# Split-SiLU-multiply on one core: the two DMA rings change their parts with every tile

## The chip, the core and the metric

The kernel runs on one core of a Trainium2 chip. Three engines of the core matter here: ScalarE (ACT), which computes the activation; VectorE (DVE), which multiplies; and SyncE (SP), which only issues transfers. SyncE and ScalarE can each issue DMA transfers, and each has a ring (a queue) of its own for them. The transfers of both rings are carried out by the core's 16 DMA engines. In the profile the ring of SyncE is q1 and that of ScalarE is q10; SPq and ACTq are the queues of instructions on these two engines.

The metric is the time of one execution on the device in microseconds (us), the median of the runs. A profile of one execution shows the span from the first to the last instruction, which is somewhat shorter than the time.

## The reference

```python
batch, seq, dim = (32, 512, 2048)
x = np.random.randn(batch, seq, dim).astype(np.float32)

half_dim = x.shape[-1] // 2
x1, x2 = x[..., :half_dim], x[..., half_dim:]
silu_x1 = x1 * (1 / (1 + np.exp(-x1)))
return (silu_x1 * x2).astype(np.float32)
```

The input has 16,384 rows of 2048 float32 numbers (134.2 MB). The output has 16,384 rows of 1024 (67.1 MB). Each number is read once and each result written once, 201.3 MB together.

## The kernel before

The rows are cut into 16 tiles of 1024 rows. A tile lies on 128 partitions with K = 8 rows on each, and the 8 rows of a partition lie side by side in memory. So a load of a whole tile (8.39 MB) moves 64 KB in one piece per partition, and a store of a whole tile (4.19 MB) moves 32 KB per partition.

There are two input buffers (`xts`) and two output buffers (`ots`); tile i uses number i % 2 of each. The work on a tile has four steps, each a small function:

- `load(i)` (line 48) fetches tile i on SyncE's ring. It must wait until the product of tile i - 2 has been made, because that product reads the same buffer.
- `silu(i, a, b)` (line 55) runs Silu on ScalarE over the first half of each row, in place, for rows a to b of each partition. It waits for the load.
- `mul(i, a, b)` (line 59) multiplies the two halves on VectorE into the output buffer. It waits for the Silu, and for the store of tile i - 2, which reads the same output buffer.
- `store(i, a, b)` (line 64) writes the result on ScalarE's ring. It waits for the product.

The order of the instructions on each engine is the order in which the code writes them (`manual_schedule`); nothing is moved by a planner. A wait holds up all that stands behind it on the same engine. So ScalarE's queue has, tile after tile, the Silu of tile i, the store of tile i (which waits for the product of tile i) and then the Silu of tile i + 1. SyncE's queue has only loads.

The two ends are written differently. The first two tiles are loaded in halves of 4 rows per partition (`load_rows`, line 51), the first half on SyncE's ring and the second on ScalarE's. Tile 0 is computed in four pieces (`FIRST`) and stored whole. The last tile is computed in three pieces (`LAST`: 2, 3 and 3 rows per partition), and then stored in the same three pieces. A last instruction on SyncE (`seen`, line 94) waits for the latest transfers and for the last product.

The main loop, after tile 0, is

```python
        silu(i, 0, K)
        mul(i, 0, K)
        store(i, 0, K)
        if i + 2 < n_tiles:
            load(i + 2)
```

so the store of tile i and the load of tile i + 2 are issued at the same time, when the product of tile i is done, and go to different rings.

Of the kernel before, what the change touches and what calls it, by code (L numbers as in the profile page):

```python
# [1 line left out]

# [4 lines left out]


K = 8

FIRST = [(0, 2), (2, 4), (4, 6), (6, 8)]

LAST = [(0, 2), (2, 5), (5, 8)]
SYNC = mybir.DependencyInfo(mybir.DependencyClass.Sync, mybir.DependencyReason.DATA)


@with_exitstack
def kernel(
    ctx: ExitStack,
    tc: tile.TileContext,  # L20
    x: bass.AP,
    out: bass.AP,
):
    nc = tc.nc
    P = nc.NUM_PARTITIONS

    x_flat = x.flatten_outer_dims()
    out_flat = out.flatten_outer_dims()
    num_rows, in_cols = x_flat.shape
    half = in_cols // 2  # L30
    dt = x_flat.dtype
    n_tiles = num_rows // (P * K)
    assert n_tiles * P * K == num_rows

    x_view = x_flat.rearrange("(n p k) d -> n p k d", p=P, k=K)
    out_view = out_flat.rearrange("(n p k) d -> n p k d", p=P, k=K)

    in_pool = ctx.enter_context(tc.tile_pool(name="in_pool", bufs=1))
    out_pool = ctx.enter_context(tc.tile_pool(name="out_pool", bufs=1))
    xts = [in_pool.tile([P, K, in_cols], dt, name=f"xt{j}") for j in range(2)]  # L40
    ots = [out_pool.tile([P, K, half], dt, name=f"ot{j}") for j in range(2)]

    ctx.enter_context(tc.manual_schedule())

    dmas = []

    def load(i):
        dmas.append(nc.sync.dma_start(out=xts[i % 2], in_=x_view[i]))

    def load_rows(queue, i, a, b):  # L50
        dmas.append(queue.dma_start(out=xts[i][:, a:b], in_=x_view[i][:, a:b]))  # L51

    def silu(i, a, b):
        x1 = xts[i % 2][:, a:b, :half]
        nc.scalar.activation(out=x1, in_=x1, func=mybir.ActivationFunctionType.Silu)  # L55

    def mul(i, a, b):
        xt = xts[i % 2]
        return nc.vector.tensor_mul(  # L59
            out=ots[i % 2][:, a:b], in0=xt[:, a:b, :half], in1=xt[:, a:b, half:]  # L60
        )

    def store(i, a, b):
        dmas.append(nc.scalar.dma_start(out=out_view[i][:, a:b], in_=ots[i % 2][:, a:b]))

    for i in range(2):
        load_rows(nc.sync, i, 0, K // 2)
        load_rows(nc.scalar, i, K // 2, K)  # L70

    for i in range(n_tiles - 1):
        if i == 0:
            for a, b in FIRST:
                silu(0, a, b)
                mul(0, a, b)
            store(0, 0, K)
            load(2)
            continue
# [6 lines that stand above are left out]
    i = n_tiles - 1  # L86
    for a, b in LAST:
        silu(i, a, b)
        last_mul = mul(i, a, b)
    for a, b in LAST:  # L90
        store(i, a, b)


    seen = nc.sync.nop()
    for ins in [*dmas[-12:-1], last_mul]:
        tc.add_manual_dep(seen.ins, ins.ins.name, SYNC, reason="the closing waits")


# [1 line left out]
_INS = ['x']  # L100
_OUTS = [((32, 512, 1024), 'float32')]


# [23 lines left out]
```

## Time and profile before

| what | value |
|---|---|
| time, median of 3 runs | 471.64 us (471.51 to 471.64) |
| time of the profiled execution | 471.56 us |
| its span | 469.6 us |
| VectorE busy | 139.5 us, 30% of the span |
| ScalarE busy | 114.2 us, 24% |
| moved by DMA | 201.34 MB, 429 GB/s over the span |
| Silu of a whole tile | 7.03 us (14 of them) |
| product of a whole tile | 8.69 us (14 of them) |
| load of a whole tile, issue to landing | 42.2 us (14 of them) |
| store of a whole tile, issue to landing | 42.4 us (15 of them) |
| ScalarE idle until a load has landed | 340.9 us, 16 times |

How to read it: the page shows busy time of the engines, then the span in 40 equal slices, where each digit is the busy share in tenths; the row DMA is the mean busy share of the 16 DMA engines. The DMA queues are listed with their packets, megabytes and the time of their packets as a share of the time of 16 engines. The chain that ended last is followed back from the last instruction: at each step to what released it. A table of stretches gives, for each stretch of time, the busy time of each engine, the DMA share and the rate in GB/s. A transfer is counted there where its packets begin, so a short stretch can show a share a little above 1.

### The profile page before, as it was taken

How to read it: one execution, taken by the hardware profiler on the slowest of the kernel's cores; microseconds unless marked ns; L12 is line 12 of the kernel's file. 1: busy time of each engine (PE TensorE's matmuls, PEld its weight loads, DVE VectorE, ACT ScalarE, POOL GpSimd, SP SyncE). 2: the span in 40 equal slices, each digit the busy share in tenths (PEclk: the TensorE clock that was granted, in tenths of full speed). 3: DMA queues.
4: the chain of work that ended last, by engine and by line, in shares of the span. 5: the costliest groups of instructions: out<-in, count | busy, mean ns of one | idle time of the engine just before them, and what ended most of it. 6: DMA issues, size and time to landing. Idle time of an engine off the chain costs nothing.

```text
span 469.6 us, 198 instructions
## 1 busy us (share of the span) xinstructions
DVE 139.5 (30%) x21; ACT 114.2 (24%) x22; POOL 0.2 (0%) x4
## 2 busy tenths in 40 slices
DVE  0070702407034070330704307042070510605152
ACT  1053205041050410505005050050501405014060
POOL 0000000000000000000000000000000000000000
DMA  8999999999999999999999999999999999999998
GB/s 357 444 419 433 402 447 463 430 402 444 421 474 402 424 424 491 402 405 444 491 402 402 447 480 413 402 441 419 480 402 424 424 491 402 402 447 486 408 402 357
DMA packets 5185, 201.34 MB, mean 429 GB/s; under 512 B 576, under 2 KB 576, under 8 KB 576
## 3 DMA queue, kind: packets, MB, share of 16 engines
q1 hardware_dynamic: 2304, 125.83, 62.2%
q10 hardware_dynamic: 2880, 75.50, 37.3%
q14 instruction: 1, 0.01, 0.0%
HBM read 134.22 MB, written 67.11 MB: 429 GB/s over the span
## 4 chain that ended last, share of the span: by engine, by line
DMA 72%; DVE 14%; ACT 11%; DVEq 1%; issue 0%; ACTq 0%
DMA xt<-in_x_dram 72%; DVE ot L59 14%; ACT xt L55 11%; DVEq L122 1%; ACTq L51 0%; ACTq L55 0%
## 5 line engine op out<-in xcount | busy, mean ns | idle before, releaser
L59 DVE TENSOR_TENSOR ot<-xt 128x8192 f32<-128x8192 f32 (+2 forms) x21 | 139.5, 6659 | 321.3 <-ACT xt L55 321.3
L55 ACT ACTIVATE xt<-xt 128x8192 f32<-128x8192 f32 (+2 forms) x21 | 112.9, 5400 | 340.9 <-DMA xt<-in_x_dram 340.9
L55 ACT ACT_TABLE_LOAD x1 | 1.3, 1283 | 1.6 <-PEq L111 1.6
L111 POOL MEMSET const-bfloat16-1.0<- 128x1 bf16 x1 | 0.1, 102 | 0.0
L111 POOL MEMSET const-uint8-127<- 128x1 uint8 x1 | 0.1, 102 | 0.0
L111 POOL MEMSET const-float32-0.0<- 128x1 f32 x1 | 0.1, 99 | 0.2 <-issue 0.2
L111 POOL MEMSET const-float32-1.0<- 128x1 f32 x1 | 0.1, 99 | 0.0
## 6 DMA issues: line engine op xcount, KB each, us to landing
out_dram<-ot ACTq DMA_DIRECT2D x15, 4096.0 KB, 42.4
xt<-in_x_dram ACTq DMA_DIRECT2D x2, 4096.0 KB, 31.6
xt<-in_x_dram SPq DMA_DIRECT2D x2, 4096.0 KB, 31.4
out_dram<-ot ACTq DMA_DIRECT2D x2, 1536.0 KB, 7.8
out_dram<-ot ACTq DMA_DIRECT2D x1, 1024.0 KB, 7.7
xt<-in_x_dram SPq DMA_DIRECT2D x14, 42.2
```

The lines of the kernel that those rows point to most:

```text
L55: nc.scalar.activation(out=x1, in_=x1, func=mybir.ActivationFunctionType.Silu)
L59: return nc.vector.tensor_mul(out=ots[i % 2][:, a:b], in0=xt[:, a:b, :half], in1=xt[:, a:b, half:])
L111: nc = _bacc.Bacc("TRN2", target_bir_lowering=False, num_devices=1)
L122: with _tile.TileContext(nc) as tc:
```

## The change

A function `ring(i)` names two rings for tile i: for an even tile SyncE's for the store and ScalarE's for the load, for an odd tile ScalarE's for the store and SyncE's for the load. `load` and `store` use it. The first loads in halves (`load_rows`) and the order of the calls stay as they are.

```diff
     def load(i):
-        dmas.append(nc.sync.dma_start(out=xts[i % 2], in_=x_view[i]))
+        dmas.append(ring(i)[1].dma_start(out=xts[i % 2], in_=x_view[i]))
...
+    def ring(i):
+        return (nc.sync, nc.scalar) if i % 2 == 0 else (nc.scalar, nc.sync)
+
     def store(i, a, b):
-        dmas.append(nc.scalar.dma_start(out=out_view[i][:, a:b], in_=ots[i % 2][:, a:b]))
+        dmas.append(ring(i)[0].dma_start(out=out_view[i][:, a:b], in_=ots[i % 2][:, a:b]))
```

Since i and i + 2 are both even or both odd, the store of tile i and the load of tile i + 2, issued together, still go to different rings. For odd tiles both stay on the ring that they had. For even tiles they are exchanged: the loads of tiles 2, 4, 6 .. 14 go to ScalarE's ring and the stores of tiles 0, 2 .. 14 to SyncE's. Each ring then has loads and stores in turn. The last tile, 15, is odd: its stores stay on ScalarE's ring, and its load on SyncE's.

ScalarE's queue has, for an even tile i, the Silu, then the load of tile i + 2 (which waits for the product of tile i), then the Silu of tile i + 1. For an odd tile it is as before. SyncE's queue has store 0, load 3, store 2, load 5 and so on, up to load 15 and store 14.

## The prediction

> **What bounds the kernel now.** I read the busy shares and the 40 slices first, then the DMA queues, the chain that ended last, the waits, and last a table of stretches with the DMA rate of each.
>
> ```profile
> DVE 139.5 (30%) x21; ACT 114.2 (24%) x22; POOL 0.2 (0%) x4
> ...
> DMA  8999999999999999999999999999999999999998
> ...
> DMA packets 5185, 201.34 MB, mean 429 GB/s; under 512 B 576, under 2 KB 576, under 8 KB 576
> ...
> q1 hardware_dynamic: 2304, 125.83, 62.2%
> q10 hardware_dynamic: 2880, 75.50, 37.3%
> ...
> DMA 72%; DVE 14%; ACT 11%; DVEq 1%; issue 0%; ACTq 0%
> ```
>
> No engine is over 30% busy, while the DMA engines are at nine tenths or more in all slices but the first and the last. The two rings' packet times add to 62.2 + 37.3 = 99.5% of sixteen engines' span: 469.6 x 0.005 = 2.3 us is all that the engines stand idle, start and end included. q1 is SyncE's ring and q10 ScalarE's. The packet counts fit the code. One transfer is 128 packets (one per partition) and 16 small ones of a few bytes. A full load's packet is 8 rows x 8 KB = 64 KB, a half load's 32 KB, a full store's 8 x 4 KB = 32 KB. So q1 has 16 transfers x 144 = 2304, and q10 20 x 144 = 2880. Packet time per byte is the same on both rings: 62.2 / 125.83 = 0.494% per MB and 37.3 / 75.50 = 0.494%.
>
> The chain of waits names loads, but a load is not late because anything on SP or ACT is late:
>
> ```profile
> 349.01 42.20 DMA xt<-in_x_dram
> 391.20 0.02 issue
> 391.22 0.02 ACTq L55
> 391.24 0.04 issue
> 391.29 7.04 ACT xt L55
> 398.32 0.02 issue
> 398.35 8.70 DVE ot L59
> 407.05 0.02 issue
> 407.07 42.39 DMA xt<-in_x_dram
> ```
>
> A load issued at 349.01 lands 42.20 us later, then Silu 7.04 and the product 8.70, and the next but one load goes out at 407.07: 58.06 us for two tiles, 29.03 for one. Since loads go out every 29.03 us and take 42.2, each finds 42.2 - 29.03 = 13.2 us of older work in the rings. That is the margin with which the DMA engines are kept fed, and it is the number that a change of the rings would have to use up.
>
> The stretches (columns: stretch and length in us, DVE, ACT and POOL busy us, clock, DMA share, GB/s):
>
> ```profile
> 41.00:44.30 3.30, 0.00 (x0) 2.02 (x1) 0.00 (x0) 1.00 1.01 318
> 44.30:47.93 3.63, 0.00 (x0) 3.63 (x1) 0.00 (x0) 1.00 1.00 433
> ...
> 100.00:158.00 58.00, 17.38 (x2) 14.06 (x2) 0.00 (x0) 1.00 1.00 434
> ...
> 332.00:390.00 58.00, 17.38 (x2) 14.06 (x2) 0.00 (x0) 1.00 1.00 434
> 390.00:448.00 58.00, 17.39 (x2) 14.06 (x2) 0.00 (x0) 1.00 1.00 434
> 448.00:458.30 10.30, 6.45 (x3) 7.22 (x3) 0.00 (x0) 1.00 0.96 413
> ```
>
> Every two tiles run at 434 GB/s, whatever the ACT and DVE do. The one dip inside the run is the first row, of which more below. How the two rings share the engines is in the queues' view of the stretch 100 to 158 us:
>
> ```profile
> q1 hardware_dynamic: 288, 16.78, 66.7%
> q10 hardware_dynamic: 288, 8.39, 33.6%
> ```
>
> In two tiles each ring had 288 packets served, 64 KB ones on q1 and 32 KB ones on q10. So the engines take one packet from each ring in turn, by packets and not by bytes, and load(i+2) and store(i), issued together with 128 data packets each, run side by side and end together (42.2 and 42.4 us to landing).
>
> **The change part by part.** The bytes, the number of transfers and the size of each packet stay as they are. Only the ring of an even tile's transfers changes: seven loads (2, 4 .. 14) move from SP's queue to ACT's, eight stores (0, 2 .. 14) from ACT's to SP's. Odd tiles stay.
>
> Issue work. An issue of these takes 0.33 us on SP and 0.36 us on ACT (timeline at 407.07). ACT has eight fewer stores and seven more loads, so about 0.36 us less; SP has one issue more. ACT stands idle 340.9 us for loads by the table of waits and SP's queue does nothing else, so this is hidden by those waits: 0.
>
> Waits on the queues. On ACT, load(i+2) of an even tile stands where store(i) stood, behind silu(i) and ahead of silu(i+1), and waits for the same product mul(i). silu(i+1) behind it is released by its load some 13 us after that product (mul(13) ends at 407.05, and silu(14) starts at 420.36), so it is held no longer than before: 0. On SP, the order becomes store(0), load(3), store(2), load(5) .. load(15), store(14); each waits for the product of its own or, for a load, two tiles earlier, and these products end in just that order, so nothing stands behind a later one: 0. The closing wait sits on SP behind store(14), whose product ends at 436.11, 33 us before the end: 0.
>
> Order inside the rings. Before, load(i+2) queued behind load(i+1) and store(i) behind store(i-1). Now, for even i, load(i+2) queues behind store(i-1) on ScalarE's ring and store(i) behind load(i+1) on SyncE's. load(i+1) and store(i-1) are the pair that runs side by side and ends together, so the new front of each ring comes free at the same moment as the old one, to within a packet (2.42 us for 64 KB: 65,536 B x 16 over 434 GB/s). A shift of 2.4 us against a margin of 13.2 us leaves the engines fed: 0. The first loads, two halves on each ring, are untouched and balanced, so the start gives no offset.
>
> The end. store(14) moves behind load(15) on SP's ring and no longer stands ahead of the last tile's stores. From about 448 us on 2 x 4.19 MB are left whichever way, 19.3 us at 434 GB/s. One ring alone now carries them at 413 GB/s (row above), so at most 10.3 x (1 - 413/434) = 0.5 us is to be had from serving two rings. The row's ends cut packets, so I take 0, and keep -0.5 for the range. Against a loss: the last piece (1.5 MB, 3.6 us at 434 GB/s) is issued at 460.8 and lands 7.8 us later, at 468.6; less its own 3.6 us, other work covers the engines until 465.0, 4 us after that issue, and this sum of bytes is the same in either order.
>
> The dip at 41 us. In that row sixteen 64 KB packets, load(2)'s first on each engine, took 3.30 us and not 2.42: 0.88 us lost, once. load(2) goes to the other ring now. Its price in the new place has no row: it may vanish (-0.88), stay (0), or come once for each ring, since load(3) is now the first 64 KB load of SyncE's ring (+0.88). I take 0, the value of the row as it stands, and keep both ends.
>
> Sum: 0 + 0 + 0 + 0, against the profiled execution: span 469.6 plus 1.96 around it gives its 471.56, which is 0.08 under the median of the runs, 471.64. So about 471.6, with -0.88 - 0.5 = -1.4 and +0.88 as the ends of the unknown terms.
>
> A rule speaks against the change. By the Trainium skill's page "Perfetto Trace Analysis", section "DMA Optimizations", it may help to give inputs to one issuing engine and outputs to another, which is what the kernel does before; by the rows 288 and 288 the separation buys nothing here, and by that rule the sum would be the second rival's.
>
> **The rivals.** First, slower: a ring pays each time its packets grow from 32 to 64 KB. The dip at 41 us is the only place where this happens before, on q1, and it cost 0.88 us. After, each of the fourteen loads from 2 to 15 follows a 32 KB transfer on its own ring: thirteen more, 13 x 0.88 = 11.4 us, 483.0 (or, if only every second one pays, 6 x 0.88 = 5.3, 476.9). It decides from the second occurrence on, 0.88 us being 0.19%. For it: the coincidence of place and size. Against it: the engine itself goes from 32 to 64 KB with every packet pair at 434 GB/s, and load(2) is singular otherwise too, as the first transfer issued in mid-run (33.56 us). Chance 0.07.
>
> Second, slower: a load is held up by the store ahead of it, as that rule has it. The rings would have to fall out of step by more than the margin of 13.2 us. A whole tile out of step is 29.0 us, so 29.0 - 13.2 = 15.8 us of idle engines at each such load, 487.4 with one. Against it: equal packet counts in every pair, which put the rings in step again at each transfer's end. Chance 0.04.
>
> Third, faster: the dip vanishes and the two rings fill the end: 471.6 - 1.4 = 470.2, or 0.3%. For it, the rows 318 and 413; against it, the 2.3 us of idle time are mostly start-up and the closing wait, which stay. Chance 0.03.
>
> **How the numbers follow.** A measurement of this kernel can tell about 0.2% (0.94 us) from no change. No change beyond that has 0.86, at 471.6: all its terms are hidden by a margin that the trace shows. Faster has 0.03 and slower 0.07 + 0.04 = 0.11. The range 470.7 to 472.6 is that of the likeliest case: the median with -0.9 and +0.9 for the dip's two ends. It leaves out about 0.14 in the rivals.
>
> **What would show it.** Right: q1 has 17 x 144 = 2448 packets and 100.66 MB, q10 19 x 144 = 2736 and 100.66 MB, their shares about 50% each, every two tiles again at 434 GB/s, loads 42 us to landing and the chain's steps of 58.06 us. The first rival shows as a rate near 318 GB/s for 3.3 us at the start of each load, and a two-tile step over 58.06; the second as slices of the DMA row under 9 and loads landing after more than 55 us. The prediction is wrong if the rate in the two-tile stretches is not 434.

## The result: 3.1% slower, and the profile after

The changed kernel takes 485.88 us (median of 4 runs, 485.17 to 488.15) against 471.57 us for the kernel before on the same chip: a ratio of 1.0313, with a 95% interval of 1.0297 to 1.0329. That is 14.3 us more. The profiled execution took 485.17 us with a span of 483.2 us, 13.6 us over the span before.

From the page of the changed kernel:

```profile
DVE 139.5 (29%) x21; ACT 114.2 (24%) x22; POOL 0.2 (0%) x4
...
DMA  8999999999999999999999999999999999999997
...
DMA packets 5184, 201.33 MB, mean 417 GB/s; under 512 B 576, under 2 KB 576, under 8 KB 576
...
q10 hardware_dynamic: 2736, 100.66, 49.7%
q1 hardware_dynamic: 2448, 100.66, 49.1%
...
DMA 73%; DVE 13%; ACT 11%; DVEq 1%; issue 0%; ACTq 0%
```

The packets, the bytes and their split over the rings are those that the prediction gave. The engines compute for as long as before. The DMA engines are still busy nearly all the time, and yet they move 417 GB/s and not 429. The shares say how: the packets' time is now 49.7 + 49.1 = 98.8% of 483.2 us, or 477.4 us; before it was 99.5% of 469.6, or 467.3. So 10.1 of the 13.6 us are packets that took longer, and the idle time went from 2.3 to 5.8 us for the other 3.5. A high busy share hid the loss: a DMA engine that is held up in a packet counts as busy.

The chain of waits of the changed kernel shows where it enters:

```profile
59.12 42.41 DMA xt<-in_x_dram
101.52 0.02 issue
101.54 7.04 ACT xt L55
108.58 0.02 issue
108.61 8.70 DVE ot L59
117.31 0.02 issue
117.32 44.35 DMA xt<-in_x_dram
...
177.48 44.85 DMA xt<-in_x_dram
```

Silu and product are the same 7.04 and 8.70 us. The first of these loads still takes 42.41 us; those issued at 117.32 and 177.48 take about 2 us longer, and the step of two tiles is 177.48 - 117.32 = 60.16 us and not 58.06.

The stretches of two tiles, which the prediction wanted at 434 GB/s, run at 408 to 428:

```profile
100.00:158.00 58.00, 17.38 (x2) 14.06 (x2) 0.00 (x0) 1.00 1.01 425
...
332.00:390.00 58.00, 17.39 (x2) 14.06 (x2) 0.00 (x0) 1.00 0.98 408
```

The table of stretches, one tile (29.05 us) each, first of the kernel before and then of the changed one (columns as above):

```profile
71.00:100.05 29.05, 8.69 (x1) 7.03 (x1) 0.00 (x0) 1.00 1.00 433
100.05:129.10 29.05, 8.69 (x1) 7.03 (x1) 0.00 (x0) 1.00 1.01 435
129.10:158.15 29.05, 8.69 (x1) 7.03 (x1) 0.00 (x0) 1.00 1.00 433
```

```profile
71.00:100.05 29.05, 8.69 (x1) 7.03 (x1) 0.00 (x0) 1.00 1.00 433
100.05:129.10 29.05, 8.69 (x1) 7.03 (x1) 0.00 (x0) 1.00 1.04 431
129.10:158.15 29.05, 8.69 (x1) 7.03 (x1) 0.00 (x0) 1.00 0.99 428
158.15:187.20 29.05, 8.69 (x1) 7.03 (x1) 0.00 (x0) 1.00 0.98 399
```

The stretch from 71 to 100 us starts just after both rings have changed direction, and runs at the full 433 GB/s. The first turn costs nothing; the rate falls only behind later ones.

The trace also holds each packet with its ring, size and times, but not its DMA engine. The order on one engine is put together from this: each packet begins where the one before it on that engine ended. This is the sequence on one DMA engine at the turn near 100 us and at the next one near 131 us (start in us, ring, size, duration in us; 64 KB is a load, 32 KB a store, 4 B the packet that reports a transfer's completion):

```
 96.81 q1     64 KB 2.42
 99.22 q10    32 KB 1.21
100.43 q1      4 B  0.01
100.43 q10     4 B  0.01
100.44 q1     32 KB 1.49
101.93 q10    64 KB 3.66
105.58 q1     32 KB 1.21
106.79 q10    64 KB 2.42
...
127.33 q1     32 KB 1.21
128.54 q10    64 KB 2.42
130.95 q1      4 B  0.01
130.96 q10     4 B  0.01
130.96 q1     64 KB 2.42
133.38 q10    32 KB 1.21
```

The engine takes a packet from q1 and from q10 in turn, with q1 first. When the rings change their parts, the order of directions must slip: at one turn it is load, store, completions, store, load, and at the next it is store, load, completions, load, store. Here two stores in a row cost 0.28 us on the second store and 1.24 us on the load behind it; two loads in a row cost nothing.

Over all packet records around a turn, the time of each beyond the usual 2.42 or 1.21 us of its size, as a mean over the 16 engines, gives the loss. The six turns with two stores between 100 and 415 us lost 1.27, 1.75, 2.04, 1.27, 1.48 and 1.58 us, together 9.4 us, and the turns with two loads 0.0 each. Another 0.65 us lie on loads near 447 us, where no ring turns; the runs don't explain these. Together that is 10.0 of the 10.1 us of longer packets.

Of the 3.5 us of added idle time, 2.0 lie at the six turns as well, mostly between the second store and the load behind it. The other 1.5 lie at the end, because the engines, in step before, drift apart: before they end within 0.6 us of each other (467.8 to 468.4 us), after within 2.8 us (479.3 to 482.1).

### The profile page after: what moved, and what is told of

It is laid out like the page before. It is cut to its first block, busy times and chain, and to the rows that moved or that the text cites. A ratio compares the mean times of both kernels' runs of the same rounds, so it can differ in the third digit from the quotient of the medians.

```text
span 483.2 us, 180 instructions
## 1 busy us (share of the span) xinstructions
DVE 139.5 (29%) x21; ACT 114.2 (24%) x22; POOL 0.2 (0%) x4
## 3 DMA queue, kind: packets, MB, share of 16 engines
q10 hardware_dynamic: 2736, 100.66, 49.7%
q1 hardware_dynamic: 2448, 100.66, 49.1%
## 4 chain that ended last, share of the span: by engine, by line
DMA 73%; DVE 13%; ACT 11%; DVEq 1%; issue 0%; ACTq 0%
DMA xt<-in_x_dram 73%; DVE ot L59 13%; ACT xt L55 11%; DVEq L126 1%; ACTq L51 0%; ACTq L55 0%
## 6 DMA issues: line engine op xcount, KB each, us to landing
xt<-in_x_dram ACTq DMA_DIRECT2D x7, 44.4
```

## The experiments

### Packet sizes, directions or completions

The rival that came nearest in the prediction said that a ring pays when its packets grow from 32 to 64 KB. Two pairs of kernels separate size from direction. The first pair makes all packets of the main loop 32 KB:

```diff
-        dmas.append(nc.sync.dma_start(out=xts[i % 2], in_=x_view[i]))
+        dmas.append(nc.sync.dma_start(out=xts[i % 2][:, : K // 2], in_=x_view[i][:, : K // 2]))
...
-        silu(i, 0, K)
-        mul(i, 0, K)
+        rows = K if i < 2 else K // 2
+        silu(i, 0, rows)
+        mul(i, 0, rows)
```

and the same on the changed kernel. In both, the last tile is computed in two pieces of 2 rows.

> Loads from tile 2 on fetch 4 of 8 rows (packets of 32 KB, as the stores); Silu and product from tile 2 on work on 4 rows; rings as in the kernel before. Bytes: 16.8 + 14 x 4.19 + 67.1 = 142.6 MB, at 434 GB/s 329 us, and the 6 us by which the kernel before exceeds its bytes: about 335 us under the theory of packet sizes (a ring or engine pays when packets grow from 32 to 64 KB) and under that of directions (two stores in a row and then a load cost about 2 us). The theory of completions (a transfer behind a store on the same ring waits some 2.4 us after the store's last packet, and only a 64 KB packet of the other ring covers it) may give up to 14 x 1.2 = 17 us more already here.

> The same with half loads, the rings alternating as in the changed kernel. Packet sizes: equal to the kernel of half loads with the rings of before (difference 0 +- 1 us), since all packets have 32 KB. Directions: 6 or 7 places with two stores in a row and then a load stay, about 2 us each, so +12 to +14 us. Completions: every transfer behind another on its ring is covered by only a 32 KB packet, 1.2 us, so a loss at every one of the 14 turns, +14 us or more.

Measured: 336.25 us and 357.05 us. With all packets of one size the alternating rings cost 20.8 us, more than with two sizes. So packet size isn't the cause. It is also more than the 12 to 14 us of the theory of directions. Of the 22.1 us between the two profiled spans only 9.2 are longer packets; the rest is idle DMA engines. The chain of waits of the alternating kernel shows why: stores now land so late that the product waits for its output buffer (75.9 us in six waits, and none in the other kernel).

```profile
90.55 36.32 DMA out_dram<-ot
...
131.51 37.26 DMA out_dram<-ot
...
173.42 37.58 DMA out_dram<-ot
```

The second pair keeps sizes and rings and makes loads of the stores:

```diff
     def store(i, a, b):
+        if i < n_tiles - 1:
+            src = x_view[i][:, : K // 2].rearrange("p k (c d) -> p (k c) d", c=2)
+            dmas.append(ring(i)[0].dma_start(out=ots[i % 2], in_=src))
+            return
```

> The stores of tiles 0 to 14 are replaced by loads of the same 32 KB per partition into the output buffer (the output is thus not written but for the last tile); rings as in the kernel before. Same bytes, packets and turns: 471 to 473 us under every theory.

> The same, loads in place of the stores of tiles 0 to 14, rings alternating as in the changed kernel. Packet sizes: the sequence 64, 32, 32, 64 KB on each engine stays, so +14 us over the same kernel with the rings of before, about 486. Directions and completions: no store is left in the run but the last tile's, so no loss, 471 to 473.

Measured: 471.37 us and 471.33 us. The same rings, sizes, completions and turns cost nothing if everything is a load:

```profile
DMA packets 5184, 201.33 MB, mean 429 GB/s; under 512 B 576, under 2 KB 576, under 8 KB 576
...
q1 hardware_dynamic: 2448, 100.66, 49.8%
q10 hardware_dynamic: 2736, 100.66, 49.7%
```

So stores are needed for the loss. Size is out, and direction or completion of stores is left.

### Which ring, and whether a ring that turns pays

Four kernels: the parts exchanged for good (`ring` returns `(nc.sync, nc.scalar)` for every tile); stores that write half of the partitions, with the rings of before; and the changed kernel with only the even tiles' stores, or only the odd tiles', made into loads (the condition in the edit above becomes `i % 2 == 0`, or `i % 2 == 1 and i < n_tiles - 1`).

> All stores on SyncE's ring and all loads from tile 2 on ScalarE's, for every tile; nothing alternates. Theory of turns (a ring loses time at a transfer of the other direction than the one before it on that ring, about 0.9 us at each of the changed kernel's thirteen later tile turns): one turn only, at 41 us on SyncE's ring, as the kernel before has one on ScalarE's: 471 to 472. A theory that it matters which ring carries loads or stores: some us more, up to the changed kernel's 485.

> Rings as in the kernel before; stores write only the first 64 partitions (4 packets on each engine beside 8 of a load), so each engine serves some loads in a row in every tile, and half of the output is not written. Bytes 134.2 + 33.5 = 167.8 MB, at 434 GB/s 387 us plus the 6 us of the kernel before: 392 to 394 under the theory of turns (only one turn in the run). Theory of rows (an engine loses about 0.9 us where packets of one direction follow each other and then the other direction comes): 14 such places, +13 us, about 405.

> The changed kernel with the even tiles' stores replaced by loads of the same 32 KB per partition (even tiles of the output not written): SyncE's ring has only loads, ScalarE's turns at every tile. Theory of turns: one ring turns at each of 14 turns and not two; if each turn costs, +6 to +13 us over 471.5; if only turning from loads to stores costs, a loss at every second turn alone, +6; if only turning from stores to loads, the same at the other ones. Theory of rows: no two stores in a row, so 0 to +1.

> The mirror of it: the odd tiles' stores (but the last tile's) replaced by loads, so that ScalarE's ring has only loads and SyncE's turns at every tile. Theory of turns: as for the other ring, +6 to +13 us, with the losses at the other parity of tiles if only one direction of turning costs. Theory of rows: 0 to +1.

Measured: 471.3 us for the exchange, so it doesn't matter which ring has the loads; 471.49 and 471.53 us for the two in which one ring turns at every tile. The theory that a ring pays for turning, which I held then, falls: in these two a ring changes between load and store 13 and 15 times, and nothing is lost. What they don't have, and the changed kernel has, is a store of one ring directly behind a store of the other.

The half stores took 427.23 us where 392 to 394 or 405 were expected. Its engines stood idle in part (rates of 260 and 285 GB/s in single slices), and stores of only half of the partitions may have their own limit, so its total decides nothing. Its packets show stores in a row on one ring, with only a load's completion between them, and a load of up to 1.9 us over its time behind them.

### Rows of stores without a turn, and their length

```diff
     def load(i):
-        dmas.append(nc.sync.dma_start(out=xts[i % 2], in_=x_view[i]))
+        for j in range(2):
+            dmas.append(nc.sync.dma_start(out=xts[i % 2][j::2], in_=x_view[i][j::2]))
```

> The rings of before; each load from tile 2 on is issued as two transfers, of the even and of the odd partitions, with the same 64 KB packets. The completion of the first half takes a turn of SyncE's ring in mid-transfer, so that two packets of the store follow each other there, with no change of direction on any ring. Theory of store rows: at least one row of two stores in each of 14 tiles, 2 us each, +28 us (+14 to +56). Theory of rings that turn: no ring turns, 471 to 472.

Measured: 487.02 us, +15.4, with the rings of before and no ring that turns. The extra completion makes SyncE's ring miss a turn, and the directions slip as in the changed kernel. So the turn of the rings isn't needed. The size of it, 1.1 us a tile, is at the low end of what was expected, and the packets show that not all of it is rows of stores: of 13.1 us of longer packets between 43 and 440 us some 8 lie on the last of two or three loads in a row, just ahead of a store. That part has no counterpart in the changed kernel, where two loads in a row cost 0.0.

Nor does every row of two stores cost here. Around the completion of a load's first half, two stores and the load behind them lost 0.5 us on average (some 9 such rows on each engine). Around the completion of the second half, the same packets in the same order lost 0.0 us (some 12 rows). So the order of directions shows where time can be lost, but it doesn't alone decide whether it is.

> The rings change their parts with every fourth tile: three changes in the run. In the changed kernel each engine takes the packets at a change from even to odd as store, load, load, store and at the other as load, store, store, load. Theory of store rows (two stores in a row on an engine and then a load cost about 2 us; two loads in a row nothing): two of the three changes here have two stores in a row, +4 us, about 475.5, with the losses near the first and the third change and none at the second. Theory of rings that turn (both rings changing direction at once): +1 us at each of the three, 474.5, the second one too.

Measured: 475.03 us, +3.4, between the two numbers. But the kernel wasn't the clean test it was meant to be. Its rings are chosen by the tile of the load, so around each change a store and the load issued with it share one ring and the other runs dry. Stores then come eight in a row on one ring. The packets where the first such row meets the loads behind it lost 0.5 us, those of the second row 0.0, so a long row of stores alone need not cost. The last of the eight loads between the two rows, just ahead of a store, lost 1.2 us (at 127 us). From 170 to 455 us, where the other two changes are, nothing was lost, and another 2.3 us are engines idle behind 450 us. So the total lies between the two numbers by chance and decides nothing. The clean version is the next section's first.

The last pair shortens the stores of tiles 0 to 14:

```diff
     def store(i, a, b):
+        b = b if i == n_tiles - 1 else K // 2
```

> The rings of before; the stores of tiles 0 to 14 write 4 of 8 rows (packets of 16 KB, 128 of them; half of the output is not written). Bytes 134.2 + 31.5 + 4.2 = 169.9 MB, at 434 GB/s 391.4 us, plus the 6 us of the kernel before: about 397 under every theory.

> The same stores of 16 KB packets with the rings alternating as in the changed kernel. If the number of stores in a row counts, the loss stays: +14 us over the same stores with the rings of before. If it is how long an engine goes without a load packet (two of 16 KB take 1.2 us, as one of 32 KB does in the kernel before), no loss: 0 to +1 us.

Measured: 400.84 and 401.01 us, a difference of 0.17 us. (Both are 4 us over the estimate; some 2 us of that are engines idle near the end, the rest isn't explained.) With 16 KB stores the alternating rings cost nothing, though two stores still follow each other at every second turn.

### One change of parts, and what lies between two stores

```diff
-        dmas.append(ring(i)[1].dma_start(out=xts[i % 2], in_=x_view[i]))
+        dmas.append(ring(i - 2)[1].dma_start(out=xts[i % 2], in_=x_view[i]))
...
-        return (nc.sync, nc.scalar) if i % 2 == 0 else (nc.scalar, nc.sync)
+        return (nc.sync, nc.scalar) if 5 <= i < 10 else (nc.scalar, nc.sync)
```

> Each pair of a store and the load issued with it keeps two different rings; the pairs of tiles 5 to 9 have the parts exchanged, the others as before. So one change of parts (after tile 4, at about 187 us) has two stores in a row on each engine, and one (after tile 9, at about 332 us) two loads in a row. Theory of store rows: +2 us, 473.6, all of it within some 10 us of the first change. Theory of rings that turn together: +1 us at each change.

Measured: 472.62 us against 471.62, a ratio of 1.0023 (1.0014 to 1.0033). Its stretches of one tile:

```profile
158.00:187.05 29.05, 8.69 (x1) 7.03 (x1) 0.00 (x0) 1.00 0.98 420
187.05:216.10 29.05, 8.69 (x1) 7.03 (x1) 0.00 (x0) 1.00 1.00 420
216.10:245.15 29.05, 8.69 (x1) 7.03 (x1) 0.00 (x0) 1.00 1.00 433
245.15:274.20 29.05, 8.69 (x1) 7.03 (x1) 0.00 (x0) 1.00 1.00 433
...
303.25:332.30 29.05, 8.69 (x1) 7.03 (x1) 0.00 (x0) 1.00 1.00 433
332.30:361.35 29.05, 8.69 (x1) 7.03 (x1) 0.00 (x0) 1.00 0.99 429
```

The tile behind the change at 187 us runs at 420 GB/s with its DMA share at 1.00, so its packets took longer. The first row and the last, with shares of 0.98 and 0.99, are cut by their ends: by the packets, 0.0 us were lost ahead of 186 us and at the change at 333 us. The turn with two stores lost 1.28 us a DMA engine, 0.36 of it on the second store and 0.92 on the load behind. One of the two changes costs, and it is the one that the theory of store rows names.

```diff
     def load(i):
-        dmas.append(nc.sync.dma_start(out=xts[i % 2], in_=x_view[i]))
+        h = K // 2
+        for q, a in ((nc.sync, 0), (nc.scalar, h)):
+            dmas.append(q.dma_start(out=xts[i % 2][:, a:a + h], in_=x_view[i][:, a:a + h]))
```

with `store` cut in the same way.

> Each load from tile 2 on and each store but the last tile's is cut into two halves of 4 rows, one on each ring; both rings then carry stores at the same time and loads at the same time, 16 store packets of 16 KB and 16 load packets of 32 KB on each engine in turn. If a row of stores without a load between them costs in itself when both rings have work, 14 rows cost 2 us each or more: 500 us or more. If it costs only where the completion of one store lies between two stores (theory of completions), the row of each tile begins and ends at loads: 471 to 474.

Measured: 477.29 us, +5.7, neither of the two. At the ends of its rows of 16 stores the first loads lost 0.04 us per engine in the whole run, so this row of stores is no loss in itself; but its packets are of 16 KB, the size that lost nothing in the pair above too. The 5.7 us are of another kind: 1.8 us on the last loads ahead of a row of stores, about 2 us for packets of half the size, and the rest mostly engines idle in the last 30 us (2.7 us against 0.3 in the kernel before).

The last two shorten one of the two stores that meet: `b = K // 2 if i % 2 == 1 and i < n_tiles - 1 else b` in the changed kernel, and the same with `i % 2 == 0`.

> The changed kernel with the stores of odd tiles (1 to 13) writing 4 of 8 rows (16 KB packets; that quarter of the output is not written). Without loss 471.6 - 14.7 MB / 434 GB/s = 438 to 439 us. Two stores in a row then last 0.6 + 1.2 = 1.8 us, the shorter one ahead of the completions. By the length of the row a loss between none (1.2 us, no loss) and 2 us (2.4 us): about +1 at each of 7 places, 445, and the same loss in the mirrored run. By completions the short store that ends leaves less to wait for: less loss than in the mirrored run.

> The mirror: the stores of even tiles (0 to 14) write 4 of 8 rows. Without loss 471.6 - 16.8 MB / 434 GB/s = 433 to 434 us. In a row of two stores the longer one is now ahead of the completions and the shorter one behind them. By the length of the row: the same loss as in the other run, about +7 us, 440. By completions: more loss than there, +7 to +14.

Measured: 444.05 us, 5 to 6 us over its bytes, and 448.12 us, 14 to 15 over. By the packets, the six turns with two stores lost 3.7 us with the short store ahead of the completions and 7.4 us with the long one there. (In the second run 2.1 us more lie on loads at no such turn, and 5.7 us are engines idle near its end, so its total says less than its packets.) So it isn't the length of the row alone: both rows last 1.8 us. The store that ends before the completions weighs more than the one that begins behind them.

By the Trainium skill's page "DMA: Bandwidth & Descriptors", section "Queues, rings and completion order", the write that reports a completion lands only after every earlier write of that DMA engine, across its queues. That would make the completions wait for the store just ahead of them, and the two runs agree in direction; no run here shows that wait itself. In the trace the completions' packets last 0.01 us each and the next store begins at once; the time is lost on that store and on the load.

What stands after sixteen runs: in the changed kernel 9.4 of the 10.1 us of longer packets stand where a store packet, the completions, another store packet and then a load follow each other, on engines that serve both rings, and a single such turn costs by itself. The loss falls with the size of the stores, and to nothing at 16 KB. Three things are open: why a load behind the completions hides it and a store doesn't; why in the kernel with loads cut in two some 12 of 21 rows of two stores cost nothing; and whether the loss on the last load ahead of a store, which the kernels with loads cut in two and with a change every four tiles show, is the same one. A row of exactly two 32 KB stores with no completion between them could not be made with two rings, because in these kernels only a completion lets a ring miss its turn.

## Why the prediction was wrong

**What bounds the kernel, right.** The DMA engines set the time before and after, the margin of 13.2 us was not what gave way (the load issued at 117.32 us has its first packets near 131 us), and the counts and shares of packets came out as given. Issue work, waits on the queues and the closing wait cost nothing, as said: the Silu and product steps of the chain are the same to 0.01 us.

**Order inside the rings, costed at 0, is the step that failed.** The step let the new front of each ring come free "to within a packet" and asked only whether that could leave the engines without work for want of transfers. It could not. But it took 434 GB/s as a property of the engines, whatever the order of packets. Exchanging the parts of two rings that are served strictly in turn makes directions slip by one, and every second slip puts two stores together: 1.27 to 2.04 us of longer packets each, 9.4 us over six, and 2.0 us of idle engines at the same places. The rest of the 13.6 us of span is engines that fall out of step and end at different times (1.5 us) and the 0.65 us near 447 us. Why two stores cost this is open; the step failed because it gave the order of packets no price. The row that could have warned was there: the two rings had equal packet counts in every tile, so the order on an engine could have been written down, and the turn load, store, store, load seen as one that the trace of before does not have. Like the dip, a term without a row, it should then have been bounded from both sides, and not set to nothing.

**The dip at 41 us, wrongly read.** It was taken for the first 64 KB packets of a ring, with a price of -0.88 to +0.88. It goes with the start of the run's stores. With loads for stores it is gone; with no store before tile 1's it moves to that one's start at 71 us. From the stretches of these two kernels, loads for all stores and then for the even ones:

```profile
41.00:44.30 3.30, 0.00 (x0) 2.14 (x1) 0.00 (x0) 1.00 1.11 477
70.00:77.26 7.26, 0.00 (x0) 6.15 (x1) 0.00 (x0) 1.00 1.01 433
```

```profile
41.00:44.30 3.30, 0.00 (x0) 1.97 (x1) 0.00 (x0) 1.00 1.11 477
70.00:77.26 7.26, 0.00 (x0) 5.85 (x1) 0.00 (x0) 1.00 0.97 361
```

The first has no dip at either place, the second its dip at 71 us (361 GB/s against 433 costs 7.26 x (1 - 361/433) = 1.2 us; by the packets 1.0). In the changed kernel the row of the dip is at full rate:

```profile
41.00:44.30 3.30, 0.00 (x0) 0.97 (x1) 0.00 (x0) 1.00 1.11 477
```

But the loss is still there, 0.85 us against 0.90 before, now on the last packets of the first loads, begun between 38.7 and 40.7 us. Since it comes once at the first store, the change left it nearly as it was, and the value taken, 0, held for the wrong reason.

**The first rival, near in size by luck and wrong in cause.** It gave 483.0 us, at a chance of 0.07. Its 13 turns of 0.88 us are in truth six of 1.3 to 2.0 and seven of nothing. Had its cause been right, the kernels with equal packet sizes would have shown no difference and the one of loads alone 14 us; they showed 20.8 and 0.

**The second rival, out.** Loads landed 44.4 us after their issue and not more than 55, so no load waited a tile behind a store. The rule of the Trainium skill's page "Perfetto Trace Analysis", section "DMA Optimizations", that it stood for, to give inputs and outputs to different issuing engines, holds here in its result, though not through a ring that is held up.

**The end, and the third rival.** Two rings at the end gained nothing that can be seen: the last slice of the DMA row fell from 8 to 7.

**The chances.** 0.86 on no change was too much: all of it rested on one untested assumption, that order doesn't matter to a saturated DMA engine.

## What to carry to other kernels

When the DMA engines are saturated, write down the order in which one engine takes the packets of its rings, and look for places where directions stop alternating; the busy share won't show them, the GB/s of a stretch will. Loads on one ring and stores on the other, for good, kept the two directions in step here whichever ring had which, and an edit that makes a ring miss one turn, even an extra completion in mid-tile, cost 3%. Such a place is where to look and not yet a price: with the loads cut in two, some 12 of 21 rows of two stores cost nothing. A dip with one cause that fits is still only a guess until something else that fits has been tried.

## What the runs showed of the hardware that was not expected

- Two 32 KB store packets in a row around completions cost a DMA engine 1.27 to 2.04 us on average in the changed kernel, mostly on the load that follows (2.42 us packets that took up to 4.3); two loads in a row cost 0.0, and two stores of 16 KB 0.0.
- The first 32 KB store of a run costs 0.4 to 1.0 us once (318 and 361 GB/s at its place in two kernels), whether it stands at 41 or at 71 us and on either ring.
- Loads alone, on rings that turn at every tile, run at the same 429 GB/s over the span as loads and stores that alternate.
- On one ring with the other empty, eight stores in a row and the loads behind them lost 0.5 us once and 0.0 once; the last of eight loads ahead of a store lost 1.2 us.
- Two 32 KB stores around the completion of half a load, with a load behind them, lost 0.5 us on average at the first half and 0.0 at the second, in one and the same kernel.
